# Encoder layer in float32: factor sums of both feed-forwards on VectorE, and the loads of rates and receptance issued behind the weights of their stream

## The chip, the cores and the metric

One core of one Trainium2 chip runs one launch of the kernel. The metric is the time of the launch on the device in microseconds. A time given as "the median" is that of several executions; the profile is one further execution, recorded by the hardware profiler.

## The reference

One layer of an encoder on a sequence of 1024 rows with 1024 features, all in float32:

```python
f = swiglu(rmsnorm(h, ffn1_pre_g), ffn1_w_gate, ffn1_w_up, ffn1_w_down)
h = h + 0.5 * rmsnorm(f, ffn1_post_g)
z = rmsnorm(h, mix_pre_g) @ w_in
mix = concat(attention(z[:, :1536]), rwkv7(z[:, 1536:])) @ w_out
h = h + rmsnorm(mix, mix_post_g)
f = swiglu(rmsnorm(h, ffn2_pre_g), ffn2_w_gate, ffn2_w_up, ffn2_w_down)
h = h + 0.5 * rmsnorm(f, ffn2_post_g)
```

`swiglu(h, wg, wu, wd)` is `(silu(h @ wg) * (h @ wu)) @ wd` with an inner width of 2816. The attention has eight heads of 64 and three dilated patterns; `rwkv7` is a scan over the sequence in both directions, whose inputs (receptance, key, value, decay, rates, gate) are columns of z.

## The kernel before, in words

**Products.** TensorE (PE in the profile) multiplies in float32r. To keep float32 accuracy each operand is split into a high half, made by ScalarE (`split`, L186: `xh`, `wh`, `zh`), and the rest, made by VectorE (L187: `xl`, `wl`, `zl`); a block then takes three matmuls: high by high, low by high, high by low.

**The feed-forward** computes gate and up together as one 2x2 block product by seven half-size products instead of eight, numbered n = 1 to 7 in `_GateUp`. Their operands are sums of the blocks. On the side of the weights, `left` (L60 to L63) makes them from four loaded blocks `raw`, on VectorE, four operations of 128x512 for each of 22 column groups j. On the side of the rows there are eight tiles of 128 rows by 1024 features (`row_tiles`); tile i of the first four (`a`) and of the last four (`b`) make a pair. `factor_sums` makes the sums of a pair in place: its early part (L339, L340) before the factor n = 3 of that pair is turned, its late part (L342, L343) after it, since L342 overwrites what n = 3 reads. Each of its instructions has 128x512 elements, in and out of SBUF. `turn_factor` (L330) turns a factor to feature-major by four transposes on TensorE into a PSUM tile `pt`, which `split` then halves. The products run in the order 1, 2 (for j = 0 and 1), then 3, then 7 and 6, then 5 and 4, and from there column group after column group.

**First feed-forward** (in `run`): the rows are loaded, normalised (`pre`, L266, with the reciprocals L246 on VectorE), the factors 1 and 2 of the first four tiles are turned, and the four products of n = 1 and 2 are issued. Then for each tile t from 4 to 7: the gain, the early sums, the turning of n = 3, the late sums. These are 16 subtracts. `products` follows: the n = 3 products, the turning of 7 and 6, and so on.

**Second feed-forward**: its first part is woven into the output projection (`out_project`, L1106). After each tile, `done(i)` finishes the row (`post`: L256, L257, store L258), `ready(i - 1)` normalises the one before and, from tile 4 on, makes its early sums, and `turn(i - 2)` turns a factor and makes the late sums: 16 subtracts again. The weights `raw` of the n = 3 products and later ones are loaded by SyncE (L284).

**Between the two** lie the projection of z, the attention and the scan. While head h of the attention runs, `project_rwkv` computes one stream of 128 columns for the scan, in the order 4, 1, 5, 2, 6, 3, 7. For a stream 4 to 7 it first loads two tiles of rates (`ra`) and one of receptance (`rr`) that earlier stages stored, then `columns` (L426) loads eight blocks of weights (`zraw`, 128x128, four buffers) and splits them, and the matmuls `zr` (L517) follow. `stream` uses the rates behind the product (L609 on GpSimd, L619 on ScalarE). The attention's own steps around it are: scores of the far pattern `s` (L649), maximum and exponential (L652 to L654), transposes `pt` (L660) and their copy `e` (L661), products with v (L667, copied in L669 and stored in L671); scores of the near patterns (L707 to L709, L712), transposes (L721), products (L728).

**What sets the order.** Each engine runs its own list of instructions in order, and waits at an instruction until its inputs are there. A scheduler builds these lists from the program's text and its own estimates; buffers and the order of the text decide how early an instruction can stand. SyncE (SP) issues nearly all loads, in one list: a load that waits holds those behind it. GpSimd (POOL) issues the stores of many results and makes some sums.

Of the kernel before, what the change touches and what calls it, by code (L numbers as in the profile page):

```python
# [13 lines left out]
OP = mybir.AluOpType  # L14
# [8 lines left out]
ATT = 1536  # L23
# [13 lines left out]
class _GateUp:  # L37
# [72 lines left out]
    def store(self, j, half, x):  # L110


        G, H = self.K.nc.gpsimd, self.H
        self.K.nc.vector.tensor_tensor(x[:, 0], x[:, 0], x[:, 1], op=OP.mult)  # L114
        H[j % 2, half] = x
        put = lambda n, y: G.dma_start(self.hid[n - 1, j // 2], y)  # L116
        sub = lambda o, a, b: G.tensor_tensor(o, a, b, op=OP.subtract)
        if (j % 2, half) == (0, 0):
# [4 lines left out]
        elif (j % 2, half) == (1, 1):  # L123
            a11, a21, a22 = H[0, 0], H[0, 1], H[1, 1]
            put(4, a22[:, 0])
            G.tensor_tensor(a22[:, 1], a21[:, 0], a22[:, 0], op=OP.add)
            put(5, a22[:, 1])
# [9 lines left out]
    def down_sums(self, m):  # L137

        G = self.K.nc.gpsimd
        t = [self.sums.tile([128, 512], F32, name="ws", tag=f"ws{q}") for q in range(4)]  # L140
# [3 lines left out]
        for n, o, a, b in ((5, b11, b12, b11), (7, b12, b22, b12), (6, b22, b22, b11), (4, b21, b22, b21)):  # L144
            G.tensor_tensor(o, a, b, op=OP.subtract)  # L145
            G.dma_start(self.ws[n - 4, m], o)
# [17 lines left out]
class _Kernel:  # L164
# [168 lines left out]

    def factor_sums(self, a, b, late=False):

        G = self.nc.gpsimd
        lo, hi = slice(0, 512), slice(512, 1024)
        if not late:
            G.tensor_tensor(a[:, lo], b[:, lo], a[:, lo], op=OP.subtract)  # L339
            G.tensor_tensor(b[:, lo], b[:, hi], b[:, lo], op=OP.subtract)  # L340
        else:
            G.tensor_tensor(b[:, hi], b[:, hi], a[:, lo], op=OP.subtract)  # L342
            G.tensor_tensor(a[:, hi], a[:, hi], b[:, hi], op=OP.subtract)  # L343

    def row_tiles(self, p):

# [152 lines left out]
    def project_rwkv(self, p, psum, x, blocks, wide=None):  # L499

        nc, V, A, T = self.nc, self.nc.vector, self.nc.scalar, self.nc.tensor
        for c0, n in blocks:
            for tag, src in (("ra", self.lr_d["a"][0][c0 - 4]), ("ra", self.lr_d["a"][1][c0 - 4]),
                             ("rr", self.rk_d[c0 - 4])) if 4 <= c0 < 8 else ():
                a = wide.tile([128, S], F32, name=tag, tag=tag)
                self.load(a, src)
                self.rates.append(a)
            if 4 <= c0 < 8:
                self.rates.append(wide.tile([128, S], F32, name="rs", tag="rr"))
            hl = self.columns(p, ATT + c0 * 128, n * 128)  # L510
            for ct in range(c0, c0 + n):
                cs = slice((ct - c0) * 128, (ct - c0 + 1) * 128)
                ps = [psum.tile([128, 512], F32, name="zr", tag="d", bufs=2) for half in range(2)]
                for half in range(2):
                    for k, (h, l) in enumerate(hl):
                        for i, (w, j) in enumerate(((h, 0), (h, 1), (l, 0))):
                            T.matmul(ps[half], w[:, cs], x[half][j][:, k, :], start=(k == 0 and i == 0),  # L517
                                     stop=(k == NK - 1 and i == 2))
                u = p.tile([128, S], F32, name="u", tag="u", bufs=1)
                y = p.tile([128, S], F32, name="us", tag="us")  # L520
                self.shift(ct, ps, u, y)
                self.stream(p, psum, ct, y)
# [945 lines left out]
```

## Time and profile before

| | |
|---|---|
| median of 3 executions | 2325.84 us (2322.16 to 2327.16) |
| profiled execution | 2320.68 us |
| span of the profile | 2318.9 us, so 1.8 us lie around it |
| mean granted TensorE clock | 0.97 |

| engine | busy us | share of the span | instructions |
|---|---|---|---|
| TensorE (PE) | 2197.6 | 95% | 15556 |
| VectorE (DVE) | 1768.7 | 76% | 2850 |
| ScalarE (ACT) | 1022.0 | 44% | 1914 |
| GpSimd (POOL) | 591.5 | 26% | 705 |

A row of the timeline reads: start in us from the start of the span, duration, engine, line, operation, output<-inputs by the program's names, size and type of each, and how many instructions the row holds; in brackets the idle time of that engine before it, and what ended it. A row of the windows has the bounds, the length, the busy time of PE, PEld (TensorE's weight loads), DVE, ACT and POOL with the number of instructions, the granted clock (1.00 is full), the DMA engines' busy share and GB/s.

### The profile page before, as it was taken

What the parts mean: (1) busy time and instruction counts of PE and PEld (TensorE: products, weight loads), DVE (VectorE), ACT (ScalarE), POOL (GpSimd) and SP (SyncE); (2) the same over time, 40 slices, a digit from 0 to 9 for tenths busy, and PEclk for the clock granted to TensorE, in tenths of its full rate; (3) what the DMA queues carried; (4) which work ended last, traced back from release to release, by engine and by line L of the source; (5) the groups of instructions that cost most, each with busy time, mean ns of one, the idle gap of its engine ahead of it and who ended that gap; (6) DMA issues with size and microseconds to landing.
All of it is one profiled execution on the core that took longest, in us unless ns stands there. A gap on an engine that the chain in (4) does not pass through costs nothing. (4 is left out here: it accounts for less than half of the span.)

```text
span 2318.9 us, 41344 instructions
## 1 busy us (share of the span) xinstructions
PE 2197.6 (95%) x15556; PEld 1781.0 (77%) x15556; DVE 1768.7 (76%) x2850; ACT 1022.0 (44%) x1914; POOL 591.5 (26%) x705
## 2 busy tenths in 40 slices
PE   6999999999999998999998899999799999999997
PEld 4788888878877676777776777776678888887886
DVE  8899999975676254577778678747899999996565
ACT  4323332354567421566654645455442333335443
POOL 6243444420000011122230111122434444441000
PEclk8999999999999999899998799999899999999999
DMA  5244544486672523555457755357445444548665
GB/s 155 94 164 169 171 148 172 146 272 193 189 224 85 203 94 90 160 165 158 131 159 184 205 156 161 114 171 260 150 139 175 150 173 145 173 158 268 196 189 179
DMA packets 345115, 387.73 MB, mean 167 GB/s; under 512 B 73298, under 2 KB 247762, under 8 KB 344916
## 3 DMA queue, kind: packets, MB, share of 16 engines
q1 hardware_dynamic: 293344, 271.71, 38.8%
q0 software_dynamic: 31216, 100.73, 11.4%
q10 hardware_dynamic: 20356, 12.66, 1.9%
q8 instruction: 122, 2.00, 0.4%
q14 instruction: 77, 0.63, 0.1%
HBM read 258.06 MB, written 126.94 MB: 166 GB/s over the span
## 5 line engine op out<-in xcount | busy, mean ns | idle before, releaser
L186 ACT ACTIVATE wh<-raw 128x512 fp32r<-128x512 f32 (+1 forms) x273 | 168.8, 627 | 268.4 <-PE gu L81 105.2
L81 PE MATMUL gu<-xh,wh 128*128 128x512 f32 x704 | 277.1, 394 | 2.1 <-ACT wh L186 1.2
L81 PE MATMUL gu<-xh,wl 128*128 128x512 f32 x704 | 275.8, 392 | 0.6 <-DVE wl L187 0.6
L81 PE MATMUL gu<-xl,wh 128*128 128x512 f32 x704 | 276.1, 392 | 0.0
L187 DVE TENSOR_TENSOR wl<-raw,wh 128x512 fp32r<-128x512 f32 (+1 forms) x273 | 273.3, 1004 | 3.4 <-ACT wh L186 2.5
L415 PE MATMUL pd<-gl,gwh 128*128 128x512 f32 x616 | 240.3, 390 | 2.4 <-DVE gl L187 2.4
L415 PE MATMUL pd<-gh,gwh 128*128 128x512 f32 x616 | 239.5, 390 | 0.6 <-DVE row L86 0.6
L415 PE MATMUL pd<-gh,gwl 128*128 128x512 f32 x616 | 239.7, 389 | 0.0
L86 DVE TENSOR_TENSOR row<-gu,row 128x512 f32<-128x512 f32 x308 | 206.5, 682 | 27.6 <-PE gu L81 25.9
L187 DVE TENSOR_TENSOR gwl<-graw,gwh 128x512 fp32r<-128x512 f32 (+1 forms) x176 | 118.0, 673 | 129.1 <-ACT gwh L186 127.5
L116 POOL DMA_DIRECT2D d_hid<-row x154 | 85.0, 553 | 476.3 <-DVE row L114 451.5
L186 ACT ACTIVATE gwh<-graw 128x512 fp32r<-128x512 f32 (+1 forms) x176 | 101.4, 576 | 190.8 <-PE pd L415 157.5
L81 PEld LDWEIGHTS gu<-xh,wh 128*128 128x128 f32 x704 | 133.5, 190 | 31.0 <-ACT xh L186 2.0
L81 PEld LDWEIGHTS gu<-xh,wl 128*128 128x128 f32 x704 | 133.3, 189 | 28.8 <-DVE wl L187 1.0
L81 PEld LDWEIGHTS gu<-xl,wh 128*128 128x128 f32 x704 | 133.3, 189 | 27.5
L415 PEld LDWEIGHTS pd<-gl,gwh 128*128 128x128 f32 x616 | 115.6, 188 | 27.5 <-DVE gl L187 3.7
L415 PEld LDWEIGHTS pd<-gh,gwh 128*128 128x128 f32 x616 | 115.5, 188 | 25.3 <-DVE row L86 1.0
L415 PEld LDWEIGHTS pd<-gh,gwl 128*128 128x128 f32 x616 | 115.6, 188 | 23.9
L94 ACT ACTIVATE row<-row 128x512 f32<-128x512 f32 x44 | 27.9, 633 | 224.1 <-DVE row L86 220.3
L187 DVE TENSOR_TENSOR gl<-raw,gh 128x512 fp32r<-128x512 f32 x160 | 114.2, 725 | 15.4 <-ACT gh L186 14.7
L145 POOL TENSOR_TENSOR ws<-ws 128x512 f32<-128x512 f32 x88 | 114.3, 1299 | 1.2
L186 ACT ACTIVATE gh<-raw 128x512 fp32r<-128x512 f32 x160 | 98.0, 621 | 31.0 <-DMA raw<-in_ffn_w_down_dram 21.0
(362 smaller groups left out, 5282.5 us busy)
## 6 DMA issues: line engine op xcount, KB each, us to landing
d_hid<-row POOLq DMA_DIRECT2D x154, 256.0 KB, 2.4
graw<-d_hid SPq DMA_DIRECT2D x132, 256.0 KB, 2.9
raw<-in_ffn_w_gate_dram SPq DMA_DIRECT2D x88, 256.0 KB, 3.1
raw<-in_ffn_w_up_dram SPq DMA_DIRECT2D x88, 256.0 KB, 3.4
ws<-in_ffn_w_down_dram SPq DMA_DIRECT2D x88, 256.0 KB, 4.3
d_ws<-ws POOLq DMA_DIRECT2D x88, 256.0 KB, 2.3
raw<-d_ws SPq DMA_DIRECT2D x88, 256.0 KB, 2.7
raw<-in_ffn_w_down_dram SPq DMA_DIRECT2D x66, 256.0 KB, 3.3
```

The lines of the kernel that those rows point to most:

```text
L81: self.K.nc.tensor.matmul(ps, a[:, k, :], b[:, k, :], start=(k == 0 and i == 0), stop=(k == 3 and i == 2))
L86: add = lambda o, x: V.tensor_tensor(o, ps, x, op=OP.add)
L94: A.activation(y[:, 0], y[:, 0], AF.Silu)
L116: put = lambda n, y: G.dma_start(self.hid[n - 1, j // 2], y)
L145: G.tensor_tensor(o, a, b, op=OP.subtract)
L186: self.nc.scalar.activation(h, src, AF.Copy)
L187: (eng or self.nc.vector).tensor_tensor(l, src, h, op=OP.subtract)
L415: T.matmul(ps[x], a[:, ts], b, start=(m == 0 and k == 0), stop=(m == NM - 1 and k == 2))
```

## The change

`factor_sums` issues its subtracts on VectorE instead of GpSimd, in both feed-forwards, 32 in all. In `project_rwkv` the loads and splits of the stream's weights stand ahead of the loads of rates and receptance.

```diff
     def factor_sums(self, a, b, late=False):

-        G = self.nc.gpsimd
+        V = self.nc.vector
         lo, hi = slice(0, 512), slice(512, 1024)
         if not late:
-            G.tensor_tensor(a[:, lo], b[:, lo], a[:, lo], op=OP.subtract)
-            G.tensor_tensor(b[:, lo], b[:, hi], b[:, lo], op=OP.subtract)
+            V.tensor_tensor(a[:, lo], b[:, lo], a[:, lo], op=OP.subtract)
+            V.tensor_tensor(b[:, lo], b[:, hi], b[:, lo], op=OP.subtract)
         else:
-            G.tensor_tensor(b[:, hi], b[:, hi], a[:, lo], op=OP.subtract)
-            G.tensor_tensor(a[:, hi], a[:, hi], b[:, hi], op=OP.subtract)
+            V.tensor_tensor(b[:, hi], b[:, hi], a[:, lo], op=OP.subtract)
+            V.tensor_tensor(a[:, hi], a[:, hi], b[:, hi], op=OP.subtract)
...
         nc, V, A, T = self.nc, self.nc.vector, self.nc.scalar, self.nc.tensor
         for c0, n in blocks:
+            hl = self.columns(p, ATT + c0 * 128, n * 128)
             for tag, src in (("ra", self.lr_d["a"][0][c0 - 4]), ("ra", self.lr_d["a"][1][c0 - 4]),
                              ("rr", self.rk_d[c0 - 4])) if 4 <= c0 < 8 else ():
                 a = wide.tile([128, S], F32, name=tag, tag=tag)
...
             if 4 <= c0 < 8:
                 self.rates.append(wide.tile([128, S], F32, name="rs", tag="rr"))
-            hl = self.columns(p, ATT + c0 * 128, n * 128)
```

VectorE at the start of the first feed-forward, from the L62 of the first column group on, before (`xl1_171` is the low half of the n = 3 rows, `pt_389` and the like their transposed tiles, `wl_496` the low half of the first n = 3 weight, made from `raw_223`, which L63 ends):

```order
L62 TENSOR_TENSOR raw_221<-s_490,raw_221 128x512
L60 TENSOR_TENSOR s_516<-raw_512,raw_514 128x512
L63 TENSOR_TENSOR raw_223<-raw_223,raw_221 128x512
L61 TENSOR_TENSOR raw_512<-raw_227,raw_512 128x512
L62 TENSOR_TENSOR raw_227<-s_516,raw_227 128x512
L187 TENSOR_TENSOR wl_496<-raw_223,wh_495 128x512
L63 TENSOR_TENSOR raw_229<-raw_229,raw_227 128x512
L187 TENSOR_TENSOR xl1_171<-pt_389,xh1_170 128x4x128
```

The same place now, from the same L62:

```order
L62 TENSOR_TENSOR raw_221<-s_490,raw_221 128x512
L342 TENSOR_TENSOR row_196<-row_196,row_200 128x512
L187 TENSOR_TENSOR xl1_171<-pt_389,xh1_170 128x4x128
L343 TENSOR_TENSOR row_200<-row_200,row_196 128x512
L187 TENSOR_TENSOR xl1_171<-pt_406,xh1_170 128x4x128
L342 TENSOR_TENSOR row_197<-row_197,row_201 128x512
L187 TENSOR_TENSOR xl1_171<-pt_423,xh1_170 128x4x128
L343 TENSOR_TENSOR row_201<-row_201,row_197 128x512
L342 TENSOR_TENSOR row_198<-row_198,row_202 128x512
L340 TENSOR_TENSOR row_199<-row_199 128x512
L343 TENSOR_TENSOR row_202<-row_202,row_198 128x512
L187 TENSOR_TENSOR xl1_171<-pt_440,xh1_170 128x4x128
```

An L342 and the L63 of the first column group follow there. The splits of the n = 3 rows now stand ahead of that L63, with late sums between them; before, both column groups' weight sums stood ahead of them. The eight early sums but this L340 stand ahead of this place, among the gains L266.

VectorE at the start of the second feed-forward, behind the gain of the last row tile, before (`s_17482` and the `raw` tiles are the first column group's weight sums, `t6l` the low half of the n = 6 rows):

```order
L187 TENSOR_TENSOR xl1_16694<-pt_17413,xh1_16693 128x4x128
L60 TENSOR_TENSOR s_17482<-raw_17478,raw_17480 128x512
L187 TENSOR_TENSOR xl1_16694<-pt_17443,xh1_16693 128x4x128
L61 TENSOR_TENSOR raw_17478<-raw_17474,raw_17478 128x512
L62 TENSOR_TENSOR raw_17474<-s_17482,raw_17474 128x512
L187 TENSOR_TENSOR t6l_17463<-pt_17534,t6h_17462 128x4x128
L63 TENSOR_TENSOR raw_17476<-raw_17476,raw_17474 128x512
```

And now:

```order
L339 TENSOR_TENSOR row_16487<-row_16483,row_16487 128x512
L187 TENSOR_TENSOR xl1_16694<-pt_17422,xh1_16693 128x4x128
L340 TENSOR_TENSOR row_16483<-row_16483 128x512
L187 TENSOR_TENSOR xl1_16694<-pt_17413,xh1_16693 128x4x128
L342 TENSOR_TENSOR row_16483<-row_16483,row_16487 128x512
L187 TENSOR_TENSOR xl1_16694<-pt_17429,xh1_16693 128x4x128
L343 TENSOR_TENSOR row_16487<-row_16487,row_16483 128x512
L187 TENSOR_TENSOR xl1_16694<-pt_17436,xh1_16693 128x4x128
L60 TENSOR_TENSOR s_17482<-raw_17478,raw_17480 128x512
L187 TENSOR_TENSOR xl1_16694<-pt_17443,xh1_16693 128x4x128
L61 TENSOR_TENSOR raw_17478<-raw_17474,raw_17478 128x512
```

The four sums of the last pair stand between the splits; behind this piece the weight sums of both column groups come first, and the `t6l` split behind the first L63.

SyncE at the start of the attention, before and now (`qp`, `kp`, `v`, `vn` and `far` belong to the attention):

```order
L182 DMA qp<-d_q 128x1024
L182 DMA kp<-d_kt 64x1024 x2
L182 DMA ra<-d_a_116 128x1024
L182 DMA ra<-d_a_119 128x1024
L182 DMA rr<-d_rk 128x1024
L182 DMA zraw<-in_w_in_dram 128x128 x4
L182 DMA kp<-d_kt 64x1024 x2
L182 DMA vn<-d_va 128x8x128
L182 DMA far<-d_n_104 128x8x66
```

```order
L182 DMA qp<-d_q 128x1024
L182 DMA kp<-d_kt 64x1024 x2
L182 DMA zraw<-in_w_in_dram 128x128 x4
L182 DMA ra<-d_a_116 128x1024
L182 DMA ra<-d_a_119 128x1024
L182 DMA zraw<-in_w_in_dram 128x128 x4
L182 DMA rr<-d_rk 128x1024
L182 DMA kp<-d_kt 64x1024 x2
L182 DMA far<-d_n_104 128x8x66
L182 DMA vn<-d_va 128x8x128
```

Eight weight loads moved ahead of `rr`, four of them ahead of `ra`. On ScalarE, three `zh` splits now stand ahead of L654 and a fourth behind it, and the copy L661 stands ahead of both L619; on PE, four zr matmuls stand between L649 and L660, three more behind L660. This is the stream of head 0; the loads of the streams 5, 6 and 7 stand as before.

## The prediction

> **What bounds the kernel now.** I read the profile page first, for busy shares and the chain of work that ended last, then windows of busy time to find where PE waits, and last the timeline of each engine in those stretches.
>
> ```profile
> PE 2197.6 (95%) x15556; PEld 1781.0 (77%) x15556; DVE 1768.7 (76%) x2850; ACT 1022.0 (44%) x1914; POOL 591.5 (26%) x705
> ...
> PE 34%; DVE 5%; DMA 3%; issue 1%; ACT 1%; POOL 1%; SPq 0%; ACTq 0%; DVEq 0%; POOLq 0%
> ```
>
> ```profile
> core 0: us, PE busy (x) PEld busy (x) DVE busy (x) ACT busy (x) POOL busy (x), PEclk, DMA share, GB/s
> 0.00:60.00 60.00, 37.56 (x136) 27.64 (x136) 49.70 (x59) 29.32 (x55) 40.28 (x43) 0.89 0.57 154
> 60.00:120.00 60.00, 56.09 (x256) 45.67 (x257) 49.84 (x63) 23.10 (x41) 16.12 (x19) 0.94 0.30 101
> 116.00:174.00 58.00, 58.00 (x257) 48.02 (x256) 57.22 (x63) 16.48 (x30) 26.08 (x30) 1.00 0.48 164
> ...
> 925.00:950.00 25.00, 17.63 (x138) 13.47 (x139) 10.87 (x25) 11.49 (x27) 2.35 (x1) 0.58 0.67 193
> 950.00:975.00 25.00, 25.00 (x271) 20.22 (x269) 16.77 (x46) 15.72 (x43) 4.69 (x6) 1.00 0.58 143
> ...
> 1640.00:1680.00 40.00, 30.49 (x143) 24.17 (x142) 33.18 (x43) 17.62 (x34) 26.85 (x16) 0.83 0.54 169
> ```
>
> TensorE is busy 95% of the span, so little can be won anywhere but in the 5% where it waits or runs at a lowered clock. The change touches three such places: the start of the first feed-forward (37.56 of 60 us busy), the start of the attention (17.63 of 25 us, granted clock 0.58) and the start of the second feed-forward (30.49 of 40 us). Right behind them PE is full: 58.00 of 58.00 us from 116, 25.00 of 25.00 from 950. A PE that is full passes on unchanged whatever it was handed earlier or later, so I cost each place by how much sooner PE gets through the work there. One caution goes with the second row: VectorE too is busy 57.22 of 58.00 us there. No sum is moved into that stretch.
>
> **Place A, first feed-forward: the 16 subtracts.**
>
> ```profile
> 25.80 1.71 POOL L339 TENSOR_TENSOR row<-row 128x512 f32<-128x512 f32 x1 [2.99 <-DVE rs L246]
> ...
> 53.12 1.60 POOL L343 TENSOR_TENSOR row<-row 128x512 f32<-128x512 f32 x1
> ...
> 34.66 1.78 DVE L62 TENSOR_TENSOR raw<-s,raw 128x512 f32<-128x512 f32 x1
> ...
> 44.72 1.74 DVE L63 TENSOR_TENSOR raw<-raw 128x512 f32<-128x512 f32 x1
> 46.39 1.27 DVE L187 TENSOR_TENSOR xl<-pt,xh 128x512 fp32r<-128x512 f32 x2
> ...
> 57.01 0.68 DVE L187 TENSOR_TENSOR wl<-s,wh 128x512 fp32r<-128x512 f32 x1
> 57.61 0.68 DVE L60 TENSOR_TENSOR s<-raw 128x512 f32<-128x512 f32 x1
> ...
> 36.37 1.03 PE L330 MATMUL pt<-ident,row 128*128 128x128 f32 x8
> 47.12 1.97 PE L330 MATMUL pt<-ident,row 128*128 128x128 f32 x8 [9.72 <-DVE xl L187]
> 49.92 1.22 PE L81 MATMUL gu<-xh,wh 128*128 128x512 f32 x2 [0.84 <-ACT xh L186]
> ...
> 60.39 1.22 PE L330 MATMUL pt<-ident,row 128*128 128x128 f32 x8 [1.07 <-DVE xl L187]
> 62.52 0.63 PE L330 MATMUL pt<-ident,row 128*128 128x128 f32 x4 [0.91 <-DVE xl L187]
> 62.90 0.48 PE L81 MATMUL gu<-xh,wh 128*128 128x512 f32 x1
> ```
>
> GpSimd makes the sums from 25.80 to 54.72 us. In exactly that stretch VectorE's 128x512 operations with both inputs in SBUF take 1.74 to 1.78 us; behind it they take 0.68 and start 0.60 apart (57.01, 57.61). Operations that read a PSUM tile keep 0.60 apiece inside the stretch too (46.39: two in 1.27). So VectorE pays about 1.1 us for each two-SBUF operation that meets GpSimd, and PE waits 9.72 us at 47.12 for a split that stands behind them.
>
> Now by hand, in the order of the changed program, a slot being 0.60 us. From 25.70 VectorE does seven subtracts (L339, L340), three 128x1024 gains (two slots each) and L60 to L62: 16 slots, 9.6 us, with a reciprocal done at 35.4. The first L342 overwrites what the transposes at 36.37 read, so it starts at 36.95; the transposes do not move, since PE is in its first products until then. Then follow, in slots: L342, xl, L343, xl, L342, xl, L343, L342, L340, L343, xl, L342, L63. L63 is the thirteenth: it ends at 36.95 + 13 x 0.60 = 44.75. ScalarE's half of that weight adds 0.62 and some latency, and the first n=3 product starts at about 45.55 instead of 49.92: 4.4 us sooner. In the remaining way to the first n=7 product (62.90) PE loses its waits of 1.07 and 0.91 us, because the splits of the n=7 columns now stand ahead of the later weights' splits; with some transposes drawn into the products I get 55.7 there. **Term A: -7.3 us**, between -4 (only the first product's lead, the rest taken back while the sixth and fifth factors are turned) and -10 (the whole of the 9.72 us wait).
>
> **Place C, second feed-forward: the other 16.**
>
> ```profile
> 1643.47 2.15 POOL L339 TENSOR_TENSOR row<-row 128x512 f32<-128x512 f32 x1 [22.00 <-DVE row L266]
> ...
> 1671.16 1.27 POOL L343 TENSOR_TENSOR row<-row 128x512 f32<-128x512 f32 x1
> ...
> 1657.50 2.04 DVE L257 TENSOR_TENSOR row<-row,res 128x1024 f32<-128x1024 f32 x1 [0.19 <-DMA res<-d_h]
> ...
> 1666.89 1.72 DVE L60 TENSOR_TENSOR s<-raw 128x512 f32<-128x512 f32 x1 [0.45 <-DMA raw<-in_ffn_w_up_dram]
> 1671.57 0.69 DVE L187 TENSOR_TENSOR xl<-pt,xh 128x512 fp32r<-128x512 f32 x1 [2.96 <-ACT xh L186]
> ...
> 1674.22 0.68 DVE L63 TENSOR_TENSOR raw<-raw 128x512 f32<-128x512 f32 x1
> ...
> 1669.79 1.97 PE L330 MATMUL pt<-ident,row 128*128 128x128 f32 x8 [4.71 <-POOL row L340]
> ...
> 1676.68 0.80 PE L81 MATMUL gu<-xh,wh 128*128 128x512 f32 x1 [1.20 <-ACT wh L186]
> ```
>
> Here GpSimd is itself the late one: PE waits 4.71 us for its L340. But the wait cannot all be won. The weights of the first n=3 product are loaded behind the last row's store, and that store waits for the L257 at 1657.50, which waits for its own load; its 2.04 us may fall to 1.2, its start hardly moves. The weights therefore land near 1666.9, as the wait of L60 shows. From the end of that L257, about 1659.4, VectorE has 24 slots to the L63 that PE needs: eight remaining sums, the gain, and the splits and weight sums that it does today. 24 x 0.60 = 14.4 puts L63's end at 1673.9 instead of 1674.9, the wh behind it and the product at 1674.65 instead of 1676.68. VectorE gets 16 x 0.60 = 9.6 us more; it has 6.8 idle us in this window (33.18 of 40), and collisions such as the 2.04 and 1.72 above end. **Term C: -2 us**, between +1 (one slot of order lost and the n=6 turns, which now stand behind L63, late as well) and -5 (the whole of PE's wait).
>
> What GpSimd had queued behind the sums (stores of rows, sums of the down weights) only starts sooner, or as before.
>
> **Place B, attention: the loads.**
>
> ```profile
> 927.32 0.80 SPq L182 DMA_DIRECT2D ra<-d_a x2
> ...
> 928.63 1.92 SPq L182 DMA_DIRECT2D zraw<-in_w_in_dram x4
> ...
> 928.64 0.63 ACT L654 ACTIVATE sb<-sb 128x512 f32<-128x512 f32 x1 [2.80 <-DVE sb L653]
> 930.89 0.81 ACT L619 ACTIVATE rb<-ra,ka,kah 128x512 f32<-128x512 f32 x1 [1.62 <-DMA ra<-d_a]
> 931.61 0.56 ACT L661 COPY e<-pt 128x512 f32<-128x512 f32 x1
> ...
> 929.33 1.12 PE L660 MATMUL pt<-ident,sb 128*128 128x128 f32 x4 [4.55 <-ACT sb L654]
> 932.27 0.33 PE L667 MATMUL po3s<-v,e 64*64 64x65 f32 x1 [1.83 <-issue]
> ...
> 943.05 0.80 PE L517 MATMUL zr<-xh,zh 128*128 128x512 f32 x1
> ...
> 959.76 0.39 PE L517 MATMUL zr<-xh,zh 128*128 128x512 f32 x1
> 959.99 0.39 PE L517 MATMUL zr<-xl,zh 128*128 128x512 f32 x1
> ```
>
> Only the first stream's block differs in the built order. Today the SyncE queue stands at the first `ra` until 927.32, and the stream's weights (zraw) go behind it, so the stream's first matmul runs at 943.05. After, four zraw loads go ahead of `ra`, which can start as late as before; the other four zraw, `rr` and the next head's `kp` then follow some 2 us later than today, and nothing on PE asks for them before 935. Two things follow. ScalarE no longer sits on L619, which waited 1.62 us for `ra`, ahead of L661: with the copy first, it can start when the transposes of 929.33 end, about 930.5 instead of 931.6, 1.1 us sooner. And some seven zr matmuls run in PE's waits of 4.55 and 1.83 us; each is one that PE need not do at 0.23 us (959.76 to 959.99) once it is full: 1.6 us. Seven more run in the cold stretch to 943, where I can see neither gain nor loss. **Term B: -2.5 us**, between -6 (the waits of 4.55 and 1.83 us gone) and +2 (zraw landing late, so that L660, which stands behind four zr matmuls, waits).
>
> **The sum.** -7.3 - 2.0 - 2.5 = -11.8, so the profiled execution of 2320.68 us becomes 2308.9. The median of the runs shown, 2325.84, lies 5.16 us above that execution; the same step puts the median at 2314, and I take **2313**, for the ends of A and B reach further down than up.
>
> **The rivals.**
> *VectorE's slow operations are not GpSimd's doing* (loads fill SBUF at the same time, 154 GB/s in the first window). Then the sums too take 1.67 us a slot. To keep the first n=3 product at 49.92, L63 must end about 0.8 us ahead of it, at 49.1; that leaves 23.4 us for the 29 slots from 25.70, so the point from which it decides at A is 23.4 / 29 = 0.81 us a slot. At 1.67 the slots take 48.4 us, and L63 ends at 74.1, 25 us late; with C's eight last sums (8 x 1.07 = 8.6) I get 2313 + 7.3 + 2 + 25 + 8.6, about 2355: slower. For it: the profile shows no run without GpSimd's sums. Against: 46.39 and 57.01, slow only with two SBUF inputs and only inside GpSimd's stretch. Chance 0.08. The Trainium skill, "SBUF — State Buffer", section "Who interferes with whom", says that a VectorE instruction with two SBUF inputs contends with a GpSimd one that reads SBUF; by that rule this rival is out, and the trace agrees (1.78 beside 0.68 us).
>
> *A slot costs the whole duration.* Each sum writes what the next one reads, and such pairs may not overlap: 0.69 instead of 0.60 us. Over 29 slots at A and 24 at C that is 53 x 0.09 = 4.8 us, and 2318 results. Against: the changed order puts a split between most of these pairs. Chance 0.13. The Trainium skill, "VectorE: DVE Perf Modes", section "The DRAIN you can't avoid", says that the next operation does not start until the pipe is empty; by that rule this rival is right, and the trace shows 0.60 for neighbours that don't depend on each other.
>
> *The gain is given back.* At A the sixth, fifth and fourth factors and the next weight sums are queued on VectorE behind what I moved up, and it is busy 57.22 of 58 us soon after; if PE comes to wait there, A keeps only 2 us, C and B none: 2324, no change. Chance 0.14. Against: from 60 to 120 VectorE has 10 idle us (49.84 of 60), and PE's 3.9 there are waits that can only shrink if the splits come sooner.
>
> **How the numbers follow.** The forecast has 0.65, the rivals 0.08, 0.13 and 0.14. About 0.2% (4.7 us) is what a measurement of this kernel can tell from no change. The forecast and the second rival are faster: 0.78; the third the same: 0.14; the first slower: 0.08. The ends of the terms together give -4 + 1 + 2 = -1 and -10 - 5 - 6 = -21, from 2325.84 that is 2325 and 2305; the runs shown spread over 5 us, of which I add 2 below: 2303 to 2325. That takes in the forecast's bounds and the second and third rival, and leaves out the first.
>
> **What would show it.** Right: between 26 and 55 us VectorE's L60 to L63 take 0.68 us; the first n=3 product near 45.5, the first n=7 one near 56; the second feed-forward's first n=3 product about 2 us nearer to the last L257 than today; L661 ahead of L619 and about 1 us after its transposes, and no sum left on GpSimd. Wrong: two-SBUF operations above 0.8 us without GpSimd, new PE waits on a DVE t6, t5 or weight split between 55 and 116, or a longer way from 918 to 960 than today.

## The result, and the profile after

The changed kernel takes 2308.02 us (median of 4 executions, 2306.62 to 2310.22), the kernel before 2324.65 us (4 executions). The ratio is 0.9939, with a 95% interval of 0.9914 to 0.9964: faster, by 0.4 to 0.9%; the medians lie 16.6 us apart. Two more comparisons of the same pair gave 0.9921 (0.9896 to 0.9945) and 0.9921 (0.9904 to 0.9938). The forecast was 2313 with a range of 2303 to 2325.

The profile's page of the changed kernel, busy times and chain:

```profile
PE 2202.1 (95%) x15556; PEld 1783.4 (77%) x15556; DVE 1767.4 (77%) x2882; ACT 1020.3 (44%) x1914; POOL 535.9 (23%) x673
...
PE 38%; DVE 3%; DMA 2%; ACT 2%; issue 1%; POOL 0%; SPq 0%; ACTq 0%; DVEq 0%; POOLq 0%
```

VectorE has 32 instructions more and is not busier: 1767.4 us against 1768.7. What it took over it paid for with collisions that are gone. GpSimd lost 55.6 us of work and its share of the chain.

**Place A.** Windows of the changed kernel, then two windows of the kernel before for comparison, and the timeline of the changed kernel:

```profile
0.00:60.00 60.00, 42.86 (x169) 31.26 (x169) 46.14 (x77) 32.52 (x61) 13.31 (x27) 0.91 0.54 148
60.00:120.00 60.00, 58.03 (x270) 47.59 (x269) 56.77 (x67) 20.19 (x36) 23.23 (x27) 1.00 0.38 129
...
65.00:70.00 5.00, 4.29 (x22) 3.38 (x20) 4.76 (x9) 2.02 (x4) 0.00 (x0) 1.00 0.15 43
70.00:75.00 5.00, 3.74 (x22) 2.87 (x23) 4.74 (x8) 2.01 (x4) 0.00 (x0) 1.00 0.08 23
75.00:80.00 5.00, 5.00 (x29) 4.14 (x28) 3.12 (x5) 2.32 (x4) 0.00 (x0) 1.00 0.29 85
```

```profile
75.00:80.00 5.00, 2.72 (x17) 1.77 (x15) 3.71 (x6) 2.52 (x5) 0.00 (x0) 0.88 0.36 105
80.00:85.00 5.00, 4.67 (x16) 3.81 (x17) 2.14 (x4) 1.48 (x3) 0.00 (x0) 0.50 0.00 0
```

```profile
25.69 0.68 DVE L339 TENSOR_TENSOR row<-row 128x512 f32<-128x512 f32 x1
...
36.46 0.69 DVE L342 TENSOR_TENSOR row<-row 128x512 f32<-128x512 f32 x1 [1.02 <-PE pt L330]
...
43.70 0.68 DVE L63 TENSOR_TENSOR raw<-raw 128x512 f32<-128x512 f32 x1
...
45.55 0.80 PE L81 MATMUL gu<-xh,wh 128*128 128x512 f32 x1 [1.20 <-ACT wh L186]
...
56.59 0.48 PE L81 MATMUL gu<-xh,wh 128*128 128x512 f32 x1
...
70.51 0.66 PE L330 MATMUL pt<-ident,row 128*128 128x128 f32 x4 [1.22 <-DVE t5l L187]
```

The 29 slots from 25.69 to the end of L63 at 44.38, less the wait of 1.02, took 17.7 us: 0.61 apiece. The first n=3 product starts at 45.55, as forecast, the first n=7 product at 56.59 (forecast 55.7, before 62.90). That the hundredths agree is luck: L63 ended 0.37 us sooner than counted and the product came 1.17 us behind it instead of 0.80, and two more profiles of the same kernel have 46.94 and 44.03. The windows from 65 us on show what no term had. The kernel before turns n=5 between 75 and 85 us: PE is idle for 2.61 us there, and its granted clock falls to 0.50. The changed kernel turns n=5 between 65 and 75 us: PE is idle for 1.97 us there, and the clock stays at 1.00.

**Place B.** The changed kernel, SyncE, ScalarE and PE:

```profile
911.19 2.01 SPq L182 DMA_DIRECT2D zraw<-in_w_in_dram  x4
920.55 0.80 SPq L182 DMA_DIRECT2D ra<-d_a  x2
...
923.98 0.58 ACT L661 COPY e<-pt 128x512 f32<-128x512 f32 x1 [1.00 <-PE pt L660]
...
918.82 0.80 PE L517 MATMUL zr<-xh,zh 128*128 128x512 f32 x1 [1.41 <-ACT zh L186]
...
922.83 1.11 PE L660 MATMUL pt<-ident,sb 128*128 128x128 f32 x4 [1.93 <-ACT sb L654]
...
918.50:943.50 25.00, 22.52 (x214) 17.11 (x214) 14.08 (x37) 13.87 (x36) 2.51 (x3) 0.82 0.68 202
```

The weights go out 9.4 us ahead of `ra`, the copy starts 1.15 us behind its transposes instead of 2.28, and in the 25 us that begin 6.6 us behind the projection's last matmul, as the window of before did, PE is busy 22.52 us instead of 17.63 at a granted clock of 0.82 instead of 0.58.

**Place C.** The changed kernel:

```profile
1647.35 1.23 DVE L257 TENSOR_TENSOR row<-row,res 128x1024 f32<-128x1024 f32 x1 [0.18 <-DMA res<-d_h]
...
1662.73 0.68 DVE L63 TENSOR_TENSOR raw<-raw 128x512 f32<-128x512 f32 x1
...
1664.13 0.79 PE L81 MATMUL gu<-xh,wh 128*128 128x512 f32 x1 [2.55 <-ACT wh L186]
...
1628.00:1668.00 40.00, 31.59 (x145) 25.19 (x144) 39.18 (x61) 17.83 (x36) 0.00 (x0) 0.83 0.55 177
```

From the start of the last L257 to the first n=3 product it is 16.78 us instead of 19.18: 2.4 us. VectorE is now busy 39.18 of 40 us here: PE's last wait, 2.55 us, ends with the half of the weight that L63 feeds.

### The profile page after: what moved, and what is told of

The parts are those of the page before. It is cut to its first block, busy times and chain, and to the rows that moved or that the text cites. A ratio compares the mean times of both kernels' runs of the same rounds, so it can differ in the third digit from the quotient of the medians.

```text
span 2307.0 us, 41317 instructions
## 1 busy us (share of the span) xinstructions
PE 2202.1 (95%) x15556; PEld 1783.4 (77%) x15556; DVE 1767.4 (77%) x2882; ACT 1020.3 (44%) x1914; POOL 535.9 (23%) x673
## 5 line engine op out<-in xcount | busy, mean ns | idle before, releaser
L415 PE MATMUL pd<-gl,gwh 128*128 128x512 f32 x616 | 240.4, 390 | 2.4 <-DVE gl L187 2.4
L415 PE MATMUL pd<-gh,gwh 128*128 128x512 f32 x616 | 239.6, 390 | 0.6 <-DVE row L86 0.6
L415 PE MATMUL pd<-gh,gwl 128*128 128x512 f32 x616 | 239.8, 389 | 0.0
L81 PEld LDWEIGHTS gu<-xl,wh 128*128 128x128 f32 x704 | 133.5, 190 | 27.6
L415 PEld LDWEIGHTS pd<-gl,gwh 128*128 128x128 f32 x616 | 115.7, 188 | 27.2 <-DVE gl L187 3.6
L415 PEld LDWEIGHTS pd<-gh,gwh 128*128 128x128 f32 x616 | 115.6, 188 | 25.3 <-DVE row L86 1.0
L415 PEld LDWEIGHTS pd<-gh,gwl 128*128 128x128 f32 x616 | 115.7, 188 | 24.0
L187 DVE TENSOR_TENSOR gl<-raw,gh 128x512 fp32r<-128x512 f32 x160 | 114.2, 726 | 17.5 <-ACT gh L186 17.1
```

Source lines behind the costliest of these rows:

```text
L81: self.K.nc.tensor.matmul(ps, a[:, k, :], b[:, k, :], start=(k == 0 and i == 0), stop=(k == 3 and i == 2))
L187: (eng or self.nc.vector).tensor_tensor(l, src, h, op=OP.subtract)
L415: T.matmul(ps[x], a[:, ts], b, start=(m == 0 and k == 0), stop=(m == NM - 1 and k == 2))
```

## How the places are measured

Launches of either kernel spread over 10 to 20 us, as much as the largest part brings, or more. I therefore read three distances off PE's timeline in the one profiled execution of each kernel. A: start of the span to the first matmul of the down product (L415). B: last matmul of the attention's projection (L309) to the last of the first stream (the 48th of L517). C: first matmul `pw` of `out_project` (L1074) to the first down product of the second feed-forward. "Half clock" is worked out from windows of 5 us, as twice the missing share of the granted clock, which is either 1.00 or 0.50 at any moment in these traces; for A from 35 to 130 us, for B from 900 to 960.

| kernel | A us | half clock | B us | half clock | C us |
|---|---|---|---|---|---|
| before | 476.4 | 20.4 | 50.4 | 23.9 | 530.6 |
| changed, three profiles | 466.4, 467.7, 464.3 | 10.2, 10.2, 6.8 | 44.1, 44.2, 44.1 | 10.3, 13.6, 10.2 | 529.4, 532.2, 531.7 |
| first feed-forward alone | 466.5 | 10.3 | 48.5 | 17.0 | 534.3 |
| second alone | 474.9 | 20.5 | 51.7 | 27.3 | 531.9 |
| loads alone | 475.7 | 20.5 | 43.3 | 10.3 | 533.1 |
| changed, GpSimd busy | 476.1 | 20.5 | 44.3 | 13.6 | 530.9 |
| before, one wait filled | 475.1 | 20.4 | 51.7 | 27.3 | 532.6 |
| before, two waits filled | 474.0 | 17.1 | 47.1 | 6.8 | 532.4 |

## The experiments

**The parts alone.** Three kernels, each the kernel before with one part of the change. `factor_sums` got an argument for its engine, and only one feed-forward passes VectorE:

```diff
-    def factor_sums(self, a, b, late=False):
+    def factor_sums(self, a, b, late=False, eng=None):
...
-        G = self.nc.gpsimd
+        G = eng or self.nc.gpsimd
```

First feed-forward:

> Only the first feed-forward's 16 subtracts go to VectorE; the second's stay on GpSimd and the loads stay where they were. Theory (place by place, read off the two traces): the first n=3 product starts at 45.5 us instead of 49.9, PE keeps its full clock through 75 to 86 us, and the first matmul behind the gate and up products comes 10 us sooner than before; the launch is 10 us shorter than before, 7 if the clock drop near 740 us that the changed kernel showed comes with it. Rival (the prediction's own term): 7.3 us and no more, the rest of what the traces show at this place being luck of one execution. Second rival (the whole gain belongs to the loads): no change.

Measured: 2312.23 us, ratio 0.9957 (0.9940 to 0.9973) against 2321.75. A is 466.5, 10.0 us shorter than before's and like the changed kernel's. The clock drop near 740 us came along in this execution (below).

Second feed-forward:

> Only the second feed-forward's 16 subtracts go to VectorE. Theory: the first n=3 product there starts 2 us sooner against the last L257, 1 to 1.5 us are left at the end; a launch 1 to 1.5 us shorter, which timed rounds can hardly tell from none. Rival (VectorE, now 39 of 40 us busy there, pushes the work behind it): 2 us or more longer. Second rival (PE's whole wait of 4.71 us for GpSimd was worth its length): 4 to 5 us shorter.

Measured: 2320.35 us, ratio 0.9985 (0.9968 to 1.0002): 1.4 us by the medians, and an interval from 7.4 us shorter to 0.5 longer. That rules out the first rival, but the launch alone cannot tell 1 to 2 us from none, or from the second rival's 4 to 5. The place itself can. From the last L257 to the first n=3 product it is 17.0 us here and 16.8 to 17.0 in the other four profiles of the table with these sums on VectorE, against 19.2 to 19.5 in the five with them on GpSimd: about 2.4 us, and the two groups do not overlap. At the end less is left: C is 531.9, where the five kernels of the table with these sums on GpSimd have 530.6 to 534.3 (mean 532.6); it and the changed kernel's three profiles have 529.4 to 532.2 (mean 531.3). The two ranges overlap, so the 1.3 us between the means are an estimate.

Loads, with the line `hl = self.columns(...)` moved as in the change and the sums left on GpSimd:

> Only the loads of rates and receptance go behind the stream's weights; all sums stay on GpSimd. Theory (the matmuls drawn into PE's waits raise the granted clock earlier): the stretch at half clock, 27 us long before, becomes about 12 us long, and the point where PE is full again comes 6 us sooner; a launch 6 us shorter. Rival (the prediction's term, only the waits of 4.55 and 1.83 us filled and one copy sooner): 2.5 us shorter, the stretch at half clock as long as before. Second rival (this place gains only because the first one moved it in time): no change.

Measured: 2315.71 us, ratio 0.9969 (0.9956 to 0.9983): 6.0 us by the medians, 7.2 by the ratio. B is 43.3 and its half clock 10.3 us, with A as before. The gain does not need place A, and it is not the 2.5 us of the prediction.

**GpSimd busy beside the sums.** Into the changed kernel:

```diff
+                    if t == 4:
+                        c, d = (hand.tile([128, 512], F32, name=n, tag=n, bufs=1) for n in ("bz", "bo"))
+                        nc.vector.tensor_copy(c, xr[t][:, 0:512])
+                        for _ in range(16):
+                            nc.gpsimd.tensor_tensor(d, c, c, op=OP.subtract)
```

> The changed kernel, with 16 subtracts more on GpSimd in the first feed-forward, from one tile that VectorE copies at the start of the sums into another that nobody reads; so nothing waits for GpSimd, and only its reads and writes of SBUF are there again. Theory (VectorE's operations with two SBUF inputs are held up by GpSimd's): those that meet GpSimd's take 1.7 us instead of 0.68, some 16 of them, so the first n=3 product comes about 15 us later than in the changed kernel, near 60 us, and the launch is 10 to 18 us longer than the changed kernel's 2308. Operations that read PSUM stay at 0.68. Rival (it was the wait for GpSimd's results that cost, and the 1.7 us had another cause, such as the loads): 0.68 us throughout, and the changed kernel's time but for the copy's 0.6 us.

Measured: 2315.17 us, ratio 0.9969 (0.9952 to 0.9985): 6.6 us below the kernel before, where the changed kernel lies 16.6 to 18.6 us below it in its three comparisons. That is 10 to 12 us longer than the changed kernel, the lower end of what I had said. The timeline:

```profile
25.41 24.71 POOL L1229 TENSOR_TENSOR bo<-bz 128x512 f32<-128x512 f32 x16 [3.00 <-DVE bz L1227]
...
41.92 1.52 DVE L339 TENSOR_TENSOR row<-row 128x512 f32<-128x512 f32 x1
43.36 1.52 DVE L342 TENSOR_TENSOR row<-row 128x512 f32<-128x512 f32 x1
44.81 0.68 DVE L187 TENSOR_TENSOR xl<-pt,xh 128x512 fp32r<-128x512 f32 x1
...
52.40 0.68 DVE L342 TENSOR_TENSOR row<-row 128x512 f32<-128x512 f32 x1
...
55.59 0.80 PE L81 MATMUL gu<-xh,wh 128*128 128x512 f32 x1 [1.95 <-ACT wh L186]
```

While GpSimd subtracts, VectorE's operations with two SBUF inputs take 1.52 us (0.92 right behind one that reads PSUM), the one that reads PSUM 0.68, and from 50.1 on all take 0.68. The first n=3 product comes 10 us late (I had said 15), A's half clock is 20.5 us again, and A is back at 476.1. Nothing waits for these subtracts: the collisions, with the clock that goes with them, undo the whole gain of place A. The Trainium skill, "SBUF — State Buffer", section "Who interferes with whom", says that a VectorE instruction with two SBUF inputs contends with a GpSimd instruction that reads SBUF, and not with one that only writes it. The trace agrees on the reading kind (1.52 beside 0.68 us). The next kernel is the control for the writing kind: it has `nc.gpsimd.memset(d, 0.0)` in place of the subtract.

> As the experiment with 16 more subtracts on GpSimd, but GpSimd writes a tile 16 times (memset) and reads nothing. Theory (VectorE's second SBUF input and GpSimd's reads share a way): VectorE's two-input operations stay at 0.68 us, the first n=3 product at 45.5 to 46.5 us, the changed kernel's time within 2 us. Rival (any work of GpSimd in SBUF holds VectorE up): 1.2 us or more while the memsets run, the product later by as many times 0.5 us or more as operations meet them.

Measured: 2302.51 us, ratio 0.9907 (0.9883 to 0.9931), the changed kernel's; A is 464.8. Only five of the memsets fell into the sums' time, since they need nothing from VectorE:

```profile
25.88 1.11 POOL L1229 MEMSET bo<- 128x512 f32 x2
26.95 0.79 POOL L1159 TENSOR_SCALAR a0h<-a0h 128x8 f32<-128x8 f32 x1
27.68 1.12 POOL L1229 MEMSET bo<- 128x512 f32 x2
...
25.76 1.27 DVE L266 SCALAR_TENSOR_TENSOR row<-row,rs,s_ffn_pre_g 128x1024 f32<-128x1024 f32 x1
...
27.56 0.68 DVE L339 TENSOR_TENSOR row<-row 128x512 f32<-128x512 f32 x1
28.16 1.27 DVE L266 SCALAR_TENSOR_TENSOR row<-row,rs,s_ffn_pre_g 128x1024 f32<-128x1024 f32 x1
```

The two-input operations that met one kept 0.68 and 1.27 us: writes alone did no harm to them, on the evidence of a few. The added copy L1227, which has one input, did take 0.91 us beside the first memset and 0.41 in the kernel with the subtracts, where nothing of GpSimd ran beside it; no run shows why.

**What the loads gained beyond the term: PE's clock, in part.** To the kernel before, useless matmuls are added in PE's wait ahead of the transposes of head 0. The one that needs the maxima `n3` keeps them from running earlier.

```diff
+        if h == 0:
+            w, flat = self.warm[0][0], pt.rearrange("p a b -> p (a b)")
+            T.matmul(flat[0:8, 0:8], n3[:, :, 65], n3[:, :, 65], start=True, stop=True)
+            for i in range(7):
+                T.matmul(flat, w[:, 0, 0:128], w[:, 0, :], start=True, stop=True)
```

> The kernel before, loads and sums as they were, with eight useless matmuls on PE in its wait ahead of the transposes L660 of head 0: one of 8x8 that needs the maxima of the scores, so that they cannot run earlier, and seven of 128x512 as the stream's are, into the PSUM tile that the transposes overwrite. Theory (in the loads' gain of 6 to 7 us most is clock: PE that has work in its waits is granted full speed sooner): although PE does 3 us of work for nothing, the stretch at half clock ends some 10 us sooner than before, and the way from the last matmul of the projection to the end of the first stream's product, 50.4 us before and 44 with the loads moved, becomes 46 to 48 us. Rival (the gain was the stream's own matmuls done early, and the copy freed): 50 to 51 us, half clock as long as before, the launch as before or 1 us longer.

Measured: 2324.41 us, ratio 1.0009 (0.9994 to 1.0024). B is 51.7, half clock 27.3 us: the rival's numbers. In the changed kernel the wait behind the transposes is closed too, and PE works without a gap from 10.9 to 27.6 us behind the projection. So the next kernel adds these lines ahead of the products with v:

```diff
+        if h == 0:
+            w, flat = self.warm[0][0], po[0].rearrange("p a b -> p (a b)")
+            T.matmul(flat[0:8, 0:8], s[:, 0, 0:8], s[:, 0, 0:8], start=True, stop=True)
+            for i in range(6):
+                T.matmul(flat[:, 0:256], w[:, 0, 0:128], w[:, 0, 0:256], start=True, stop=True)
```

> The kernel before with useless matmuls in both of PE's waits beside the transposes L660 of head 0: the eight ahead of them as in the experiment before this, and behind them one of 8x8 that needs the exponentials and six of 128x256, into the PSUM tile that the products with v overwrite. Theory (the clock comes back after PE has worked without a gap for longer than the 4.3 us that one filled wait gave; it is the wait behind the transposes that the moved loads closed): PE works without a gap from 8.5 to some 17 us behind the projection's last matmul, full clock is there at 16 to 18 us instead of 28, and the end of the first stream's product comes 3 to 6 us sooner than in the kernel before, 45 to 48 us behind the projection, although 5 us of PE's work is for nothing. Rival (the gain is the stream's own matmuls done in the waits and the copy freed, and the clock only follows): 50 to 52 us as before, half clock until 27 us or later.

PE's timeline (the added lines move the numbers of those behind them: L663 are the useless matmuls, L665 the transposes) and windows, of the kernel with one wait filled and then of that with two:

```profile
925.48 3.35 PE L663 MATMUL pt<-xh 128*128 128x512 f32 x7
928.63 1.05 PE L665 MATMUL pt<-ident,sb 128*128 128x128 f32 x4
...
940.00:945.00 5.00, 4.95 (x37) 3.57 (x37) 3.08 (x9) 1.95 (x6) 0.00 (x0) 0.50 0.69 187
```

```profile
929.48 3.17 PE L663 MATMUL pt<-xh 128*128 128x512 f32 x7
932.48 0.60 PE L665 MATMUL pt<-ident,sb 128*128 128x128 f32 x4
...
932.00:936.00 4.00, 2.83 (x44) 2.26 (x45) 0.38 (x1) 2.00 (x3) 0.70 (x1) 0.96 0.97 368
936.00:940.00 4.00, 3.34 (x46) 2.59 (x42) 0.57 (x2) 2.31 (x5) 1.66 (x1) 1.00 1.05 270
```

Up to the transposes the two kernels have the same instructions. In the first the transposes take 1.05 us and half clock goes on past 945; in the second they take 0.60, so full clock came back within the first filled wait, 11 us behind the projection, ahead of the lines that are new. My sentence on the wait behind the transposes is therefore not borne out: they may have kept the clock up, but they did not bring it back. What the pair does show is the price of the clock. With it up, B is 47.1 us although PE does 4 us of useless work; with it down, 51.7 us, and 48.5 to 51.7 in the four kernels whose loads stand as before. That is 1.5 to 4.6 us of the loads' 6.3; the rest goes to the stream's matmuls done in the waits and the copy. The four kernels point the same way among themselves, since B grows with the moment at which full clock comes back: 48.5 us where that is 22.4 us behind the projection, 50.4 where it is 27.4, and 51.7 twice where it is 30.8. With the loads moved it is 13.9 to 16.3. A handful of executions does not settle the shares. The launch did not show it either: 2323.05 us, ratio 0.9995 (0.9980 to 1.0010).

**Late sums later.** In the changed kernel VectorE's list still stands ahead of the first n=3 weight. The late sums feed n=6 and n=4 only, so here they leave the loops and go behind the turning of n=7:

```diff
         turn(7)
+        for i in range(4):
+            self.factor_sums(a[i], b[i], True)
         turn(6)
```

> The changed kernel with the late sums (L342, L343) of all four pairs issued behind the n=3 products and the turning of n=7, which don't read them, in both feed-forwards. Theory (what is left at both starts is VectorE's list ahead of the first n=3 weight): the first n=3 product starts at about 41 us instead of 45.5 and in the second feed-forward 2 to 3 us sooner, the turning of n=6 finds its sums done behind the products, and the launch is 3 to 6 us shorter than the changed kernel's. Rival (VectorE has the same work to the n=6 and n=5 splits either way, so PE meets it there): the first product as early, but new waits ahead of the n=6 products, and the changed kernel's time.

Measured: 2302.48 us, ratio 0.9916 (0.9893 to 0.9938), the changed kernel's (0.9921 beside it on the same chip). PE's timeline:

```profile
41.00 0.79 PE L81 MATMUL gu<-xh,wh 128*128 128x512 f32 x1 [1.21 <-ACT wh L186]
...
53.53 0.66 PE L330 MATMUL pt<-ident,row 128*128 128x128 f32 x4 [1.23 <-DVE t6l L187]
```

The product is 4.5 us sooner, and PE then waits for t6l, where it did not: A is 466.0. In the second feed-forward it is 1.5 us sooner, not the 2 to 3 that I had expected. The rival holds. In a last try the four sums of n=6 stand there, and the four of n=4 behind the turning of n=5:

> The changed kernel with the late sums behind the turning of n=7 as before, and now in two parts: the four that n=6 reads (L342) there, and the four that only n=4 reads (L343) behind the turning of n=5, in both feed-forwards. Theory (VectorE's list ahead of each factor is what PE waits for at both starts): the first n=3 product at 41 us, the waits of 1.23, 0.54 and 0.69 us ahead of the n=6 products gone, and the way to the first down product 2 to 4 us shorter than the changed kernel's; the launch 2 to 5 us shorter. Rival (the sums only meet PE at the next factor): the same waits ahead of the n=5 or n=4 products instead, and the changed kernel's time within 1 us.

Measured: 2303.40 us, ratio 0.9918 (0.9898 to 0.9939), and the changed kernel beside it 2302.68. A is 463.2, but PE still waits 1.15 us twice for t6l: the weights' splits moved into the place of the sums. No version beats the changed kernel clearly.

**The changed kernel again,** twice:

> The changed kernel itself, unaltered, beside the others on the same chip. Theory: 13 to 20 us below the kernel before, the sum of the three parts run singly (10.0, 1 to 3.5 and 6 to 7); at the attention 6 us and at the first feed-forward 10 us of it again. Rival (the parts share a gain, or the clock drop near 740 us that the changed kernel's profile showed belongs to the change): 8 to 11 us, with the drop there again.

> The changed kernel unaltered, for the comparison on the same chip. Theory: 14 to 18 us below the kernel before, and 2 to 5 us above the kernel with the late sums in two parts; rival: level with it.

Measured: 2301.88 and 2302.68 us, 18.4 and 18.6 us below the kernel before. The parts alone add up to 9.5 + 1.4 + 6.0 = 16.9 us by the medians and to 20.7 by the ratios, so they neither share a gain nor need each other, as far as launches can tell. A window of the changed kernel's first profile, and the same window of the first repetition, about which the first expectation asked:

```profile
740.00:745.00 5.00, 5.00 (x11) 2.65 (x10) 4.65 (x3) 3.80 (x6) 0.00 (x0) 0.50 0.51 210
```

```profile
740.00:745.00 5.00, 5.00 (x17) 2.76 (x17) 5.00 (x3) 4.94 (x7) 0.00 (x0) 1.00 0.45 184
```

The same code runs here once at half clock and once at full. The drop costs about 3 us, and PE has no wait above 0.1 us in the 10 us ahead of it. It stands in four of 13 profiles at the same point, 273 us behind the first down product, and in a fifth a longer one stands 32 us further on. Since the changed kernel has it in one profile of three, it is an execution's. Whether the change makes it likelier is open: the four all have the first feed-forward's sums on VectorE, as eight of the 13 do; only the fifth has them on GpSimd.

## Why the prediction was right, point by point

- **What bounds the kernel:** right. PE's waits at three places, passed on by a full PE: A's 10.1 us of the first profile are still 10.1 at 614 us, where the down product runs.
- **Term A, -7.3 us:** the mechanism was right, and shown: VectorE at 0.61 a slot, L63 and, in the first profile, the n=3 product within 0.4 us of the hand count, and the gain gone when GpSimd's reads come back. (One reading was too neat: of the two-input operations in GpSimd's stretch before, two at 47.59 and 48.19 took 0.68 us. They started in a pause of GpSimd, from 47.59 to 48.31.) Only the size was off (by its own figures 7.2, 62.90 less 55.7): 474.0 to 476.4 in the five kernels with GpSimd's sums against 464.3 to 467.7 in four profiles without, a difference of 9.0 us in the means (475.2 and 466.2). What was missing lies behind the first n=7 product: in the first profile 6.3 us were won by then and 9.0 by the first n=4 product (81.63 instead of 90.65), the difference mostly at the turning of n=5. There 3.4 or 6.8 us at half clock stand in four of the five kernels with GpSimd's sums, and none in the four profiles without.
- **Term C, -2 us:** right in mechanism and size at the place: 2.4 us to the first product, of which 0.8 is the last L257 itself, as described. What is left at the end is 1.3 us in the means of C and 1.4 in the launch, neither clear of none.
- **Term B, -2.5 us:** the weakest step. The queue, the copy freed by 1.1 us and the seven zr matmuls in the waits all came as described (1.1 and 1.6 us, whose sum is 2.7, not 2.5). It was "seven more run in the cold stretch to 943, where I can see neither gain nor loss" that failed: the stretch was not a given. Time at half clock there fell from 23.9 to 10.3 us, eleven more of the stream's matmuls, not seven, ran in the time that went up to 943 before, and the term measures 6.3 us (B of 50.4, 48.5 and 51.7 against 43.3 to 44.2), just beyond its own end of -6, which rested on the waits and not on the clock.
- **The sum, -11.8 us:** low by 5 to 7 us, 3.8 of them from B and 1.7 to 2.8 from A; the range, the sum of all ends, still took it in. That the two profiled executions differ by just 11.9 us of span (2318.9 and 2307.0) is chance: in them A gained 10.1, B 6.4 and C 1.2 us, together 17.7, and the changed one lost some 3.6 us between the first down product and the projection, where the drop near 740 us lies, and 2.3 in the attention and the scan behind place B.
- **The rivals:** the first (slow whatever GpSimd does) fell with the rows of 0.68 and with the busy GpSimd. The second (0.69 a slot) fell with 0.61. The Trainium skill, "VectorE: DVE Perf Modes", section "The DRAIN you can't avoid", by whose rule the prediction calls this rival right, goes on to say that a next operation that is not held starts earlier; the trace agrees with that (0.68 us long, 0.60 apart). The third (given back later) did not happen at A, where the waits for t5l from 70.51 on add up to 1.98 us and were 1.92 us in the kernel before; but it is just what happened to the two tries with late sums.

## What to carry to other kernels

Before moving work off an engine because it looks overloaded, compare the duration of the same operation inside and outside the other engine's stretches: VectorE here got 32 operations more and was busy for 1.3 us less. When a change fills or opens waits of a TensorE that runs at half clock, cost the matmuls behind them at both clocks, for both cases belong in the range. And where single launches spread more than the effect, read the place's own distance in several profiles.

## What the runs showed of the hardware

Half clock comes in pieces of one size. In the windows of all kernels its sum at a place is 3.4, 6.8, 10.2, 13.6, 17, 20.5, 23.9 or 27.3 us: multiples of 3.4. The Trainium skill, "TensorE: Matmul & The Clock Gate", section "Part 1: The HAM clock gate (the “warmup” mystery)", says that the clock is decided in free-running windows of about 3.4 us; the trace agrees: in each of the 13 profiles all changes of the granted clock lie on one grid of 3.41 us.

Where the grid falls differs from execution to execution, and that fits the two kernels with useless matmuls. In the first, the work from the filled wait on covers 62% and 66% of the two steps of the grid that it falls into, and half clock goes on. In the second it covers 87% of one step, which ends 11.2 us behind the projection, and full clock comes back there. It is not the whole rule: in the kernel before, PE is busy for 94% or more of each of the three steps from 17.1 to 27.4 us behind the projection, and full clock comes back only at the end of the third. No run was made to test either.

A whole profiled execution spent between 106 and 152 us at half clock. The launches' spread goes with it: of the 33 launches of the kernel before in the comparison of the parts, the shortest (2316.29 us) had a mean granted clock of 0.972, and the two longest (2332.29 and 2335.31 us) had 0.961.
